# The pooling mixer of a fused two-layer trunk: its steps, and those of the first half up blocks, listed in another order on four engines, with fewer products on zeros

## The chip, the cores and the metric

The kernel runs on one core of one Trainium2 chip, with one launch. The metric is the device time of an execution in microseconds (us), the median of several runs. Engines are called as the profile calls them: PE is TensorE (PEld its weight loads), DVE VectorE, ACT ScalarE, POOL GpSimd, SP the engine that issues the transfers.

## What is computed

A decoder trunk of two layers on x of 512 x 1024, in float32. Layer 0 mixes by causal average pooling over four windows, layer 1 by stick-breaking attention; each is followed by an MLP with squared ReLU. Only the mixer of layer 0 and the entry of its MLP matter here:

```python
POOL_WINDOWS = (2, 4, 8, 16)
def pool_mixer(h, w_grp, scale):
    ...                                   # per group of 256 channels: mean over the last w rows, minus h itself
    y = jnp.einsum('bsgc,gcd->bsgd', y, w_grp.astype(jnp.float32)).reshape(B, S, D)
    return (y * scale.astype(jnp.float32)).astype(h.dtype)
def sq_relu_mlp(h, w_up, w_down):
    u = jnp.matmul(h, w_up)
    return jnp.matmul(jnp.square(jax.nn.relu(u)), w_down)
    ...
        h = rms_norm(x, mix_pre_g[layer])
        ...
        x = x + rms_norm(m, mix_post_g[layer])
        h = rms_norm(x, mlp_pre_g[layer])
        x = x + rms_norm(sq_relu_mlp(h, w_up[layer], w_down[layer]), mlp_post_g[layer])
```

## The kernel before

The 512 rows are four tiles t = 0 to 3 of 128 rows; the 1024 channels are two halves h of 512, or eight blocks of 128. Every product with a weight is made of three products of split operands (a high and a low part of each), so that each weight and each activation passes through a copy on ACT (high) and a subtraction on DVE (low).

The mixer is written as single steps, and one list, MIX_ORDER, says in which order they are issued. Inside that list the tile scheduler is off for PE, ACT, DVE and POOL (`tc.manual_schedule`): each of the four executes its own instructions in the order of the list, and waits for the others by semaphores. SP, and everything behind the mixer, is ordered by the scheduler. A step is a letter and its arguments; `p02` is pooled(0, 2), `z3` is busy(3). The steps, with the line (of the kernel before) that the profile shows:

- `z` busy(n), L773, PE: n products of a tile of zeros (bf16, 128x512) into a bank that nobody reads.
- `r`/`e` scale_row, scale_copy, L778 PE and L781 ACT: the row of per-channel scales, spread over 128 partitions by a product with ones.
- `q`/`v` first squares of x[t] (L302, ACT) and the norm from them: two small POOL instructions, the total (L306) and the power of -1/2 (L313).
- `b` band, L810 DVE: the pooling matrices times that norm, into own[t].
- `p` pooled, L818 PE: x[t] times own[t], in three groups of blocks (3, 3 and 2); `c` its copy to y[t] on ACT (L828); `f` adds what reaches over from the tile before (L835 DVE).
- `w` linear, L789 DVE: scales into the group maps; `m` mixed, L846 PE: y[t] times the map.
- `s`/`g` squares of the mixer's output (L302 ACT) and its product with the gain (L350 DVE); `V` the norm (L306, L313 POOL); `a` the update of x[t] (L368 DVE); `S` squares of the new x[t] (L302 ACT); `W` its norm (L306, L313 POOL); `n` the normed x (L404 DVE); `t` four transposes (L412 PE); `h`/`l` the high and low part of the transposed tile, xnh (L422 ACT) and xnl (L431 DVE).
- `i`/`k` the high and low part of one of the first four up weights (L863 ACT, L867 DVE); `u` half_up: the first half of an up block, for tiles 0 and 1 alone, which needs their xnh and xnl and both parts of the weight.

```python
        def busy(n):
            for _ in range(n):
                nc.tensor.matmul(pwarm, warm[:, :P], warm, start=True, stop=True)
        def half_up(j):
            early.append((ps(), left.pop(("L", j))[1]))
            up_block(*early[j], slice(0, S // 2))
    ...
        for k in ks:                                     # up_block: 8 x 3 products of 128x256
            nc.tensor.matmul(pu[:, cols], wh[:, k, :], xnh[:, k, cols], start=k == 0, stop=False)   # L728
            nc.tensor.matmul(pu[:, cols], wh[:, k, :], xnl[:, k, cols], start=False, stop=False)    # L729
            if not last:
                low(k)                                                                              # L725
    ...
            for step, which in MIX_ORDER:
                steps[step](*which)
```

Behind the list the MLP of layer 0 begins: the second halves of the four up blocks (for tiles 2 and 3), then the down projection (L606) with the further up blocks between its products.

Of the kernel before, what the change touches and what calls it, by code (L numbers as in the profile page):

```python
# [43 lines left out]

MIX_ORDER = [
    (w[0], [int(w[1:])] if w[0] == "z" else [int(c) for c in w[1:]])
    for w in """z13 q00 q01 v0 r1 b0 q1 z3 p02 p00 v1 c02 e1 r0 c00 p01 b1 e0 p12 w0 c01 p10 c12 p11 c10 w1 m00 q2
    m01 c11 v2 s00 f10 f11 b2 q3 p21 g00 p22 s01 v3 g01 m11 c22 V0 b3 c21 f21 m10 a00 i0 g11 s11 k0 p32
    s10 p31 g10 m21 c32 c31 V1 a01 S00 f31 a11 p20 S01 a10 p30 S11 W0 m31 g21 S10 n00 c20 W1 c30 t00 f20
    n01 m20 s31 n10 h00 n11 i1 t01 l00 t11 s20 t10 f30 g31 m30 h10 k1 h01 h11 l01 s30 l10 s21 l11 i2 V3  # L50
    z6 u0 V2 g30 i3 a31 a21 S31 a30 S21 u1 g20 S30 a20 W3 S20 k2 n30 u2 W2 n31 n21 n20 t21 k3 t31 h21
    t30 h31 t20 l21 u3 h30 l31 h20 l30 l20""".split()
]


# [56 lines left out]
def trunk(ctx, tc, x, consts, grow, pw, wup, wdn, wq, wk, wv, wo, out):  # L112
    nc = tc.nc
# [623 lines left out]
    with tc.tile_pool(name="mix0", bufs=1, reuse_waits="tile") as mp:  # L737
# [29 lines left out]
        left, stats, ups, ys, own = {}, {}, {}, {}, {}  # L767
# [101 lines left out]
        def half_up(j):  # L869
# [5 lines left out]
            "b": band, "p": pooled, "c": copied, "f": reached, "m": mixed,  # L875
            "s": lambda t, h: ups[t].squares_of(h, left["m", t, h]),
            "g": lambda t, h: ups[t].product(h, left["m", t, h]),
            "V": lambda t: ups[t].first_rstd(), "a": lambda t, h: ups[t].add_part(h),
            "S": lambda t, h: ups[t].squares_of_x(h), "W": lambda t: ups[t].rstd(),
            "n": lambda t, h: ups[t].norm_part(NS[h]), "t": transposes,  # L880
# [473 lines left out]
```

## Time and profile before

| | before |
|---|---|
| device time, three runs | 946.4, 946.53, 947.62 us; median 946.53 |
| the profiled execution | 947.41 us, of which the span of its instructions is 945.6 us |
| mean granted PE clock | 0.998 |
| PE busy | 936.8 us, 99% of the span, 4702 matmuls |
| DVE, ACT, POOL busy | 696.3 (74%), 560.0 (59%), 41.1 us (4%) |
| bytes moved | 156.15 MB, 46.0% of the 16 DMA engines' span |

The span counts from the first instruction to the last; 1.8 us of the profiled execution lie around it. The mixer and the half up blocks take the first 48 us of the span. Matmuls are pipelined, so that a row's duration is longer than its distance to the next row; on PE the distances between starts are what one product costs.

### The profile page before, as it was taken

To read this page: it belongs to the slowest core of one execution; us is meant where nothing else is said; L and a number is where in the kernel's file an instruction comes from. 1 tells how busy PE (TensorE), PEld (TensorE's weight loads), DVE (VectorE), ACT (ScalarE), POOL (GpSimd) and SP (SyncE) were. 2 spreads that over 40 slices of the span, in tenths; PEclk is the share of its full clock that TensorE was granted. 3 is DMA by queue.
4 is the path that set the end of the run, shared out by engine and by line. 5 is a ranking of instruction groups with operands and counts; after the bars stand their busy time and mean duration, and the time that the engine had idled before them with its cause. 6 is when DMAs were issued, how large, how long until landed. Compare 5 with 4: busy or idle time off the path is not lost.

```text
span 945.6 us, 12346 instructions
## 1 busy us (share of the span) xinstructions
PE 936.8 (99%) x4702; PEld 789.7 (84%) x4702; DVE 696.3 (74%) x797; ACT 560.0 (59%) x983; POOL 41.1 (4%) x83
## 2 busy tenths in 40 slices
PE   9999999999999999999999999999999999999996
PEld 7998888888888888888889888898888888888885
DVE  5865799988978976268766388884696966858756
ACT  6667979788784647155545464875545444444532
POOL 2300000000000004000000001200000000000002
PEclk9999999999999999999999999999999999999999
DMA  8254969789597860633151271342514233133102
GB/s 301 96 189 132 353 212 350 292 277 364 215 322 267 292 217 2 222 134 134 63 178 73 103 276 45 138 153 91 175 45 148 75 133 112 47 132 112 42 3 90
DMA packets 43262, 156.15 MB, mean 165 GB/s; under 512 B 4289, under 2 KB 4673, under 8 KB 43202
## 3 DMA queue, kind: packets, MB, share of 16 engines
q1 hardware_dynamic: 43202, 155.36, 46.0%
q8 instruction: 37, 0.61, 0.3%
q14 instruction: 23, 0.19, 0.1%
HBM read 121.79 MB, written 33.55 MB: 164 GB/s over the span
## 4 chain that ended last, share of the span: by engine, by line
PE 97%; POOL 1%; ACT 1%; DVE 1%; issue 0%; POOLq 0%; DVEq 0%; ACTq 0%
PE ps L606 28%; PE ps L728 15%; PE ps L725 15%; PE ps L729 15%; PE ps L317 4%; PE ps L318 4%; PE ps L319 4%; PE ps L1063 2%; PE ps L1046 2%; PE ps L1088 2%; PE ps L846 1%; PE ps L412 1%; PE ps L818 1%; PE ps L773 1%; ACT xn L302 1%; DVE x L368 0%
## 5 line engine op out<-in xcount | busy, mean ns | idle before, releaser
L606 PE MATMUL ps<-w,a 128*128 128x512 f32 x1176 | 278.6, 389 | 0.0
L728 PE MATMUL ps<-xnh,w 128*128 128x512 f32 (+1 forms) x704 | 260.5, 372 | 0.0
L729 PE MATMUL ps<-xnl,w 128*128 128x512 f32 (+1 forms) x704 | 259.9, 370 | 0.0
L725 PE MATMUL ps<-xnh,w 128*128 128x512 f32 (+1 forms) x704 | 259.2, 370 | 0.1
L606 PEld LDWEIGHTS ps<-w,a 128*128 128x128 f32 x1176 | 220.7, 188 | 45.9 <-DVE w L299 0.2
L729 PEld LDWEIGHTS ps<-xnl,w 128*128 128x128 f32 x704 | 132.7, 189 | 22.2
L725 PEld LDWEIGHTS ps<-xnh,w 128*128 128x128 f32 x704 | 132.2, 188 | 22.9 <-DVE w L867 0.3
L728 PEld LDWEIGHTS ps<-xnh,w 128*128 128x128 f32 x704 | 132.3, 188 | 22.4
L615 DVE TENSOR_TENSOR y<-ps,y 128x512 f32<-128x512 f32 x124 | 84.5, 688 | 44.3 <-PE ps L606 44.2
L178 DVE TENSOR_TENSOR w<-raw,w 128x1024 fp32r<-128x1024 f32 x58 | 70.9, 1223 | 57.1 <-ACT w L176 56.9
L176 ACT CAST w<-raw 128x1024 fp32r<-128x1024 f32 x58 | 60.8, 1048 | 81.9 <-PE ps L725 80.9
L298 ACT CAST a<-r 128x768 fp32r<-128x768 f32 (+1 forms) x60 | 47.6, 794 | 71.8 <-PE ps L606 55.4
L299 DVE TENSOR_TENSOR a<-r,a 128x768 fp32r<-128x768 f32 (+1 forms) x60 | 54.1, 902 | 11.9 <-ACT a L298 11.6
L1027 DVE TENSOR_TENSOR_SCAN e<-u,begin 128x1280 f32<-128x1280 f32 x16 | 45.2, 2825 | 20.9 <-ACT u L1011 20.2
L298 ACT CAST w<-e 128x1536 fp32r<-128x1536 f32 (+1 forms) x30 | 41.8, 1395 | 23.1 <-DVE e L580 13.7
L299 DVE TENSOR_TENSOR w<-e,w 128x1536 fp32r<-128x1536 f32 (+1 forms) x30 | 49.5, 1649 | 1.8 <-ACT w L298 1.6
L188 ACT ACTIVATE apart<-apart,eye 128x128 f32<-128x128 f32 (+1 forms) x132 | 43.1, 407 | 0.0
L299 DVE TENSOR_TENSOR w<-w,w 128x1536 fp32r<-128x1536 f32 (+1 forms) x20 | 33.0, 1650 | 8.0 <-ACT w L298 7.2
L638 ACT ACTIVATE r<-ps 128x512 f32<-128x512 f32 x56 | 33.0, 589 | 9.0 <-PE ps L725 9.0
L299 DVE TENSOR_TENSOR w<-xn,w 128x1536 fp32r<-128x1536 f32 (+1 forms) x20 | 33.0, 1650 | 5.6 <-ACT w L298 5.5
L639 ACT ACTIVATE r<-r 128x512 f32<-128x512 f32 x56 | 35.5, 633 | 1.3
L302 ACT ACTIVATE xn<-y 128x512 f32<-128x512 f32 (+1 forms) x25 | 15.3, 613 | 32.2 <-DVE y L484 28.6
(134 smaller groups left out, 1327.5 us busy)
## 6 DMA issues: line engine op xcount, KB each, us to landing
raw<-in_wup SPq DMA_DIRECT2D x64, 512.0 KB, 4.1
w<-kept SPq DMA_DIRECT2D x60, 512.0 KB, 4.1
kept<-wx SPq DMA_DIRECT2D x30, 512.0 KB, 4.9
w<-in_wdn SPq DMA_DIRECT2D x8, 1536.0 KB, 6.7
kept<-apart SPq DMA_DIRECT2D x24, 512.0 KB, 5.7
xn<-in_wdn SPq DMA_DIRECT2D x8, 1536.0 KB, 7.5
apart<-in_wk SPq DMA_DIRECT2D x7, 512.0 KB, 7.2
apart<-in_wq SPq DMA_DIRECT2D x7, 512.0 KB, 9.3
```

Of the source, the lines that this page charges most:

```text
L176: nc.scalar.copy(hi, raw)
L178: nc.vector.tensor_tensor(out=lo, in0=raw, in1=hi.bitcast(F32), op=ALU.subtract)
L188: nc.scalar.mul(c, c, gc[:, at : at + 1])
L298: latest["act"] = nc.scalar.copy(hi, src)
L299: latest["dve"] = nc.vector.tensor_tensor(out=lo, in0=src, in1=hi.bitcast(F32), op=ALU.subtract)
L317: nc.tensor.matmul(dst, ah, bh, start=start, stop=False)
L606: nc.tensor.matmul(bank, a[:, x, q, TS[t]], w[:, z, q], start=start and q == 0 and k == 0, stop=q == self.n - 1 and k == 2, skip_group_che ...
L615: nc.vector.tensor_tensor(out=part, in0=bank, in1=part, op=ALU.add)
L725: nc.tensor.matmul(pu[:, cols], wl[:, k, :], xnh[:, k, cols], start=False, stop=k == KC - 1)
L728: nc.tensor.matmul(pu[:, cols], wh[:, k, :], xnh[:, k, cols], start=k == 0, stop=False)
L729: nc.tensor.matmul(pu[:, cols], wh[:, k, :], xnl[:, k, cols], start=False, stop=False)
L1027: nc.vector.tensor_tensor_scan(out=self.e[:, ::-1], data0=self.u[:, 1:][:, ::-1], data1=begin[:, ::-1], initial=0.0, op0=ALU.mult, op1=ALU ...
```

## The change

MIX_ORDER holds the same steps in another order, and of its three steps on zeros, `z13`, `z3` and `z6`, only one is left, `z11`. Two more steps, X and Y, are defined (totals on DVE in place of POOL), but the list doesn't use them. The list is one line shorter and the two definitions are two lines longer, so line numbers differ by one.

```diff
-    for w in """z13 q00 q01 v0 r1 b0 q1 z3 p02 p00 v1 c02 e1 r0 c00 p01 b1 e0 p12 w0 c01 p10 c12 p11 c10 w1 m00 q2
...
+    for w in """z11 q00 r1 q01 v0 r0 q1 b0 v1 p00 b1 p01 p02 e0 e1 c01 c00 w0 w1 c02 p10 c10 q2 p12 q3 p11 m00 v2 s00 b2 c11 f10
...
+            "X": lambda t: (ups[t].first_total(nc.vector), ups[t].first_rstd()),
+            "Y": lambda t: (ups[t].second_total(nc.vector), ups[t].rstd()),
```

The first place is PE from its first products with data to the first product of tile 1. In the names, ps is a bank of the accumulator, row and ones make the scale row, own_ and x_ with x_70 are tile 0, with x_71 tile 1. Before:

```order
L778 MATMUL ps_143<-row,ones 128x512
L773 LDWEIGHTS warm
L773 MATMUL ps_110<-warm 128x512
L773 LDWEIGHTS warm
L773 MATMUL ps_110<-warm 128x512
L773 LDWEIGHTS warm
L773 MATMUL ps_110<-warm 128x512
L818 MATMUL ps_153<-own_145,x_70 128x144 x2
L818 MATMUL ps_156<-own_145,x_70 128x144 x3
L778 MATMUL ps_165<-row,ones 128x512
L818 MATMUL ps_168<-own_145,x_70 128x144 x3
L818 MATMUL ps_175<-own_172,x_71 128x144 x2
```

The same place now:

```order
L777 MATMUL ps_138<-row,ones 128x512
L777 MATMUL ps_143<-row,ones 128x512
L817 MATMUL ps_152<-own_148,x_70 128x144 x3
L817 MATMUL ps_158<-own_148,x_70 128x144 x3
L817 MATMUL ps_162<-own_148,x_70 128x144 x2
L817 MATMUL ps_179<-own_156,x_71 128x144 x3
```

The three products on zeros are gone, and both halves of the scale row stand ahead of the pooling of tile 0; what stands ahead of the first product of tile 1 is otherwise the same.

The second place is PE at the end of the mixer, up to the first half up block. L846 (L845 now) is a mixed product, with y_243 or y_231 of tile 2 and y_277 of tile 3; L412 (L411) are the transposes of tiles 0 and 1. Before, of the six products on zeros the first alone is shown:

```order
L846 MATMUL ps39_302<-pw1_98,y3_277 128x256 x4
L412 MATMUL ps40_314<-eye_74,xn3_79 128x128 x4
L846 MATMUL ps41_321<-pw0_97,y2_243 128x256 x4
L412 MATMUL ps42_331<-eye_74,xn3_79 128x128 x4
L412 MATMUL ps43_337<-eye_74,xn3_79 128x128 x4
L412 MATMUL ps44_343<-eye_74,xn3_79 128x128 x4
L846 MATMUL ps45_350<-pw0_97,y3_277 128x256 x4
L773 LDWEIGHTS warm_85
L773 MATMUL ps3_110<-warm_85 128x512
```

And now:

```order
L845 MATMUL ps38_303<-pw1_98,y2_231 128x256 x4
L411 MATMUL ps39_316<-eye_74,xn3_79 128x128 x4
L411 MATMUL ps40_322<-eye_74,xn3_79 128x128 x4
L845 MATMUL ps42_333<-pw1_98,y3_277 128x256 x4
L411 MATMUL ps43_340<-eye_74,xn3_79 128x128 x4
L411 MATMUL ps44_348<-eye_74,xn3_79 128x128 x4
L845 MATMUL ps45_353<-pw0_97,y3_277 128x256 x4
L727 MATMUL ps46_374<-xnh_80,w5_113 128x256
```

Tile 2 is done with its mixed products before the first transposes, and the first half up block follows the last mixed product of tile 3 at once.

The third place is the update and norm of tiles 2 and 3 on DVE, whose normed x the last transposes wait for. x2_72 and stat34 or stat36 are tile 2, x3_73 and stat38 or stat41 tile 3, w7, w9 and w11 are low parts of the up weights of blocks 1, 2 and 3. Before:

```order
L350 TENSOR_TENSOR m3_300<-ps45_350,grow1_104 128x512
L368 SCALAR_TENSOR_TENSOR x3_73<-m3_300,stat38_301,x3_73 128x512
L368 SCALAR_TENSOR_TENSOR x2_72<-m2_270,stat34_271,x2_72 128x512
L368 SCALAR_TENSOR_TENSOR x3_73<-m3_300,stat38_301,x3_73 128x512
L350 TENSOR_TENSOR m2_270<-ps41_321,grow1_104 128x512
L368 SCALAR_TENSOR_TENSOR x2_72<-m2_270,stat34_271,x2_72 128x512
L867 TENSOR_TENSOR w9_119<-raw8_117,w9_119 128x1024
L404 SCALAR_TENSOR_TENSOR xn_299<-x3_73,stat38_301,spare2_106 128x512 x2
L404 SCALAR_TENSOR_TENSOR xn3_79<-x2_72,stat34_271,spare2_106 128x512 x2
```

And now:

```order
L349 TENSOR_TENSOR m3_331<-ps45_353,grow1_104 128x512
L367 SCALAR_TENSOR_TENSOR x2_72<-m2_291,stat36_292,x2_72 128x512
L866 TENSOR_TENSOR w7_116<-raw6_114,w7_116 128x1024
L349 TENSOR_TENSOR m3_331<-ps42_333,grow1_104 128x512
L367 SCALAR_TENSOR_TENSOR x3_73<-m3_331,stat41_332,x3_73 128x512 x2
L403 SCALAR_TENSOR_TENSOR xn3_79<-x2_72,stat36_292,spare2_106 128x512 x2
L403 SCALAR_TENSOR_TENSOR xn_330<-x3_73,stat41_332,spare2_106 128x512 x2
L866 TENSOR_TENSOR w11_122<-raw10_120,w11_122 128x1024
```

Tile 2 is normed before tile 3 (before, after it), and the low part of block 1's weight has moved in between, while that of block 2 now stands far ahead. On PE the transposes of tile 2 now stand behind two half up blocks and those of tile 3 behind the third, where before all four stood behind the third:

```order
L724 MATMUL ps47_401<-xnh_80,w7_116 128x256
L411 MATMUL ps48_432<-eye_74,xn3_79 128x128 x4
L411 MATMUL ps49_438<-eye_74,xn3_79 128x128 x4
L727 MATMUL ps50_443<-xnh_80,w9_119 128x256
L728 MATMUL ps50_443<-xnl_81,w9_119 128x256
```

These rows are PE's now, at the end of the second half up block; ps47 is the bank of block 1, ps50 that of block 2.

On POOL the rows of the two orders are the same ones, with the pair for tile 2 and the pair for tile 3 exchanged. On SP one transfer of down weights has moved two places forward. Behind the mixer nothing else has moved but one pair of neighbours on ACT and a few rows on DVE at the start of the down projection.

More of the change, by code (lines that the diff above doesn't have):

```diff
@@ L46 @@
     (w[0], [int(w[1:])] if w[0] == "z" else [int(c) for c in w[1:]])
-    for w in """z13 q00 q01 v0 r1 b0 q1 z3 p02 p00 v1 c02 e1 r0 c00 p01 b1 e0 p12 w0 c01 p10 c12 p11 c10 w1 m00 q2
[L48 to L52, printed above, removed]
+    for w in """z11 q00 r1 q01 v0 r0 q1 b0 v1 p00 b1 p01 p02 e0 e1 c01 c00 w0 w1 c02 p10 c10 q2 p12 q3 p11 m00 v2 s00 b2 c11 f10
+    m01 v3 p21 p20 c12 s01 b3 c21 V0 p22 f11 c20 m10 g01 g00 m11 p32 c22 a00 i0 i2 a01 s10 f20 s11 k0 p31 S00 k2
+    S01 p30 c30 g11 g10 V1 W0 a11 f21 a10 c32 n01 S11 m20 c31 n00 S10 f31 s20 m21 s21 W1 g20 g21 f30 V2 t01 n10
+    t00 n11 h00 h01 m31 l01 a20 t10 s31 l00 h10 t11 m30 l10 h11 S20 i1 l11 g30 s30 a21 S21 V3 k1 W2 g31 a30 u0
+    a31 i3 u1 n21 n20 S30 S31 W3 t21 n31 t20 u2 n30 t30 h20 k3 h21 t31 l21 h30 l20 l30 h31 l31 u3""".split()
 ]
```

## The prediction

> **What bounds the kernel now.** I read the page first, for the engine that is full and for the chain that ended last.
>
> ```profile
> PE 936.8 (99%) x4702; PEld 789.7 (84%) x4702; DVE 696.3 (74%) x797; ACT 560.0 (59%) x983; POOL 41.1 (4%) x83
> PE 97%; POOL 1%; ACT 1%; DVE 1%; issue 0%; POOLq 0%; DVEq 0%; ACTq 0%
> ```
>
> PE is busy for 99% of the span and is 97% of the chain. Busy PE is not PE at work on data, so the next view is the table by stretches, for PE alone, cut at the places where the list changes (length of the stretch, then PE busy).
>
> ```profile
> core 0: us, PE busy (x), PEclk, DMA share, GB/s
> 1.30:6.82 5.52, 5.52 (x13) 1.00 0.83 269
> 6.82:7.84 1.02, 1.02 (x3) 1.00 1.00 384
> 7.84:8.49 0.65, 0.65 (x5) 1.00 1.06 401
> 9.71:10.57 0.86, 0.86 (x4) 1.00 1.02 419
> 32.75:33.86 1.11, 1.11 (x8) 1.00 0.72 151
> 8.00:65.00 57.00, 56.95 (x390) 1.00 0.53 199
> 65.00:938.00 873.00, 872.84 (x4299) 1.00 0.46 162
> ```
>
> From 8 us to 938 us PE is idle for 0.05 + 0.16 = 0.21 us. So whatever PE time leaves the first 48 us moves all that follows forward by as much, unless PE then waits for something that the products on zeros now hide. Nothing behind the mixer waits for a fixed moment; transfers there start when buffers come free, and move along. The question is therefore a sum over PE in the first 48 us: zeros out, new waits in.
>
> **The zeros.** The timeline of PE at the start gives their price (start, length, what).
>
> ```profile
> 1.30 5.73 PE L773 MATMUL ps<-warm 128*128 128x512 bf16 x13 [1.30 <-POOL warm L739]
> 6.82 1.18 PE L778 MATMUL ps<-row,ones 128*128 128x512 f32 x2
> 7.84 0.81 PE L773 MATMUL ps<-warm 128*128 128x512 bf16 x3
> 8.49 1.39 PE L818 MATMUL ps<-own,x 128*128 128x144 f32 x10
> 9.71 1.02 PE L778 MATMUL ps<-row,ones 128*128 128x512 f32 x2
> 10.57 1.63 PE L818 MATMUL ps<-own,x 128*128 128x144 f32 x12
> ```
>
> The first thirteen take 5.52 us, 0.425 each; the next three take 0.65, 0.217 each. PE thus runs at half speed at first. The first product of the scale row takes 1.02 us and the second 0.86: the excess of 0.16 is half of 0.32 us at half speed, so the speed doubled near 6.82 + 0.32 = 7.14, 5.84 us after the first product. (The column of the granted clock reads 1.00 throughout and does not show it.)
>
> `z13` to `z11` takes out 2 x 0.425 = 0.85 us. If the speed still doubles at 7.14, that much of the scale row runs at half speed instead, so half remains: 0.43. `z3` gives 0.65. `z6` gives the 1.11 us of its stretch. Together 2.19 us, the most that the zeros can bring.
>
> **What the zeros hid at the start.** The next PE work is the pooling of tile 1, which needs own1. Its chain, from the timeline of the other engines:
>
> ```profile
> 7.62 1.06 ACT L302 ACTIVATE junk<-x 128x1024 f32<-128x1024 f32 x1 [2.72 <-DMA x<-in_x]
> 9.25 0.56 POOL L313 TENSOR_TENSOR stat<-stat,mhalf 128x1 f32<-128x1 f32 x1
> 9.85 0.52 DVE L810 TENSOR_SCALAR own<-band,stat 128x576 f32<-128x576 f32 x1 [3.35 <-POOL stat L313]
> ```
>
> It begins with the landing of x for tile 1 and ends at 9.85 + 0.52 = 10.37; the new order moves nothing ahead of it. Before, PE came to tile 1 at 10.57 plus six of the twelve rows (6 x 0.1225 = 0.74), at 11.31. Now the same work stands ahead of it, less 0.43 and 0.65: 10.23. So PE waits about 0.17 us for own1, and 0.91 of the 1.08 remain.
>
> **What z6 hid, and the waits that go.** PE's rows around the half up blocks; two starts that lie further apart than 0.12 us are a wait.
>
> ```profile
> 33.86 0.47 PE L728 MATMUL ps<-xnh,w 128*128 128x256 f32 x1
> 34.16 0.28 PE L729 MATMUL ps<-xnl,w 128*128 128x256 f32 x1
> 39.91 0.28 PE L729 MATMUL ps<-xnl,w 128*128 128x256 f32 x1
> 40.25 0.39 PE L725 MATMUL ps<-xnh,w 128*128 128x256 f32 x1
> 40.47 0.28 PE L728 MATMUL ps<-xnh,w 128*128 128x256 f32 x1
> 42.87 0.28 PE L725 MATMUL ps<-xnh,w 128*128 128x256 f32 x1
> 43.09 1.97 PE L412 MATMUL ps<-eye,xn 128*128 128x128 f32 x16
> ```
>
> From 40.47 to 42.87 twenty products take 2.40 us, 0.12 each, so a half block of 24 takes 2.88. At 34.16 PE waited 0.18 for the low part of the transposed tile 1, even behind six zeros. Without them that wait could grow by all of 1.11. But before, tile 0's second transpose also stood behind the mixed product in the middle, and ACT and DVE had three high and low parts left after the last transposes; now one group of transposes comes a mixed product earlier, and two parts remain. I take the same 0.18 as before, so no change, with bounds of 0 and +1.1. At 40.25 PE waited 0.22 for the low part of block 2's weight, which now stands far ahead, and at 43.09 0.10 for the normed x: 0.32 go. Block 1's weight has become the late one: it comes by the walk below at the moment when the second half block's third product wants it, for which I put 0.1.
>
> **The new wait: tile 2's norm.** Before, all transposes of tiles 2 and 3 stood behind three half blocks (8.6 us of cover); now those of tile 2 stand behind two. Prices for the walk, from the timelines of DVE, ACT and POOL:
>
> ```profile
> 34.13 0.68 DVE L350 TENSOR_TENSOR m<-ps,grow 128x512 f32<-128x512 f32 x1
> 38.31 0.75 DVE L368 SCALAR_TENSOR_TENSOR x<-m,stat,x 128x512 f32<-128x512 f32 x1
> 38.98 1.22 DVE L867 TENSOR_TENSOR w<-raw,w 128x1024 fp32r<-128x1024 f32 x1
> 40.95 2.74 DVE L404 SCALAR_TENSOR_TENSOR xn<-x,stat,spare 128x512 f32<-128x512 f32 x4 [0.76 <-POOL stat L313]
> 37.10 0.63 ACT L302 ACTIVATE xn<-x 128x512 f32<-128x512 f32 x1 [0.38 <-DVE x L368]
> 37.64 0.19 ACT L302 ACTIVATION_READ_ACCUMULATOR xn<-x 128x1 f32 x1
> 38.54 1.74 POOL L306 TENSOR_SCALAR stat<-stat 128x1 f32<-128x1 f32 x1 [2.31 <-ACT xn L302]
> 40.36 0.56 POOL L313 TENSOR_TENSOR stat<-stat,mhalf 128x1 f32<-128x1 f32 x1
> 40.91 0.30 POOL L306 TENSOR_SCALAR stat<-stat 128x1 f32<-128x1 f32 x1
> ```
>
> Let s be the start of the first half block. DVE has the last low part until s + 0.8, then L350 of tile 3 (0.68) to s + 1.5. ACT squares it (0.73 to the end of its second row), s + 2.2, and POOL's total of tile 3 can begin at s + 2.3. DVE then runs L368 of tile 2 and L867 of block 1, until about s + 3.25. The POOL rows show what that does: the same total takes 0.30 us at 40.91 and 1.74 at 38.54, where L368 and L867 ran beside it, and it ended at 40.28, just behind L867 (40.20). So the total ends at s + 3.35, the power (0.56) at s + 4.0. Now DVE runs the two L368 of tile 3 until s + 5.4, and POOL the total and power of tile 2. If these run undisturbed they are done by s + 5.0, and the first L404 runs from s + 5.4 to s + 6.15. If the total waits for one L368, it is done at 5.5 and L404 at 6.3; if for both, 6.2 and 7.0. PE reaches the transposes at s + 2 x 2.88 + 0.18 = s + 5.94. The wait is 0.2, 0.4 or 1.1, and the second group of four transposes waits some 0.2 more, because an L404 takes 0.68 and four transposes less. I take 0.6 + 0.2 = 0.8, between the ends 0.4 and 1.3.
>
> [...]
>
> The transposes of tile 3 have a further half block of cover, and I count nothing for them.
>
> **Edits at no cost.** X and Y are never called. The first two up weights of the MLP (L166) wait for the buffers that the split of blocks 0 and 1 frees:
>
> ```profile
> 31.88 0.33 SPq L166 DMA_DIRECT2D raw<-in_wup  x1
> 51.70 1.04 ACT L176 CAST w<-raw 128x1024 fp32r<-128x1024 f32 x1
> ```
>
> The second one goes out at 31.88, and queued behind it on SP are the loads of the down weights. With block 1's split later, it goes out some 3 us later; its user, ACT at 51.70 for the first of them, leaves more than 10 us. If that cover were gone, PE would wait for the rest of it.
>
> **The sum.** -2.19 + 0.17 - 0.32 + 0.1 + 0.8 = -1.44 us against the profiled execution of 947.41 (945.6 and 1.8 around it): 945.97. The median of the runs shown is 946.53, 0.88 below that execution, and the runs span 1.22 us. If profiling is what costs the 0.88, the forecast for a median is 946.53 - 1.44 = 945.09. If it is the moment at which PE's speed doubles, the median run had it earlier; then both orders come to tile 1 when own1 is ready, the 0.91 are lost, and -0.53 remains: 946.0. Between the two I forecast **945.7 us**.
>
> **The rivals.** About 0.2% (1.89 us) is what a measurement of this kernel can tell from no change, so faster is below 944.64 and slower above 948.42.
>
> *The speed doubles early in most runs.* Each microsecond earlier moves PE by half of it, so from 7.14 - 2 x 0.91 = 5.3 us on down PE reaches tile 1 before 10.4 in both orders, and the start brings nothing. With the wait for tile 2 at its upper end, 1.3, the sum is -0.53 + 0.5: 946.5. For it speaks the spread of the runs; against it the profiled 7.14. Chance 0.14, inside the 0.2%. [...]
>
> *The new waits do not come.* Own1 hidden because the speed rises late, the total of tile 2 undisturbed: -2.19 - 0.32 + 0.4 = -2.1, 944.4, faster. For it: most of POOL's totals run beside nothing that disturbs them, and the rows' waits at 40.25 and 43.09 were small although the same chains are long. Against: the walk puts L368 beside the total by construction. Chance 0.32.
>
> *PE loses its speed.* The zeros kept PE at work where it would wait. If the waits at the first half block and at tile 2's transposes make it fall to half speed once, for as long as it took to rise (5.84 us), that costs 2.9: 945.7 + 2.9 = 948.6, slower. [...] Chance 0.14. [...]
>
> That the zeros are not removed is excluded by the rows of the order.
>
> **How the numbers follow.** The forecast has 0.40, the early rise 0.14, the faster case 0.32, the slower one 0.14: faster 0.32, same 0.54, slower 0.14. The lower end is the median less everything, 946.53 - 2.19 - 0.32 = 944.0, with no new wait; the upper end is -0.53, with 0.5 more for tile 2 and 1.1 for the wait behind z6: 947.6. About 2 in 10 lie outside.
>
> **What would show it.** Right: PE's rows at the pooling of tile 1 start at 10.4 or later than its predecessors end; no wait at block 2's weight; a wait of 0.4 to 1.3 us ahead of the transposes behind the second half block, with a POOL total beside L367 that takes over 0.5; the first L606, which the chain shows at 64.91 before, 0.5 to 1.9 earlier, and the same distance at the end.
>
> ```profile
> 64.91 2.72 PE ps L606 x12
> ```
>
> Wrong: a distance between products of 0.24 us and not 0.12 after 10 us (the speed fell), a wait over 0.5 at the first half block, or a PE wait behind 65 us that was not there.

## The result, and the profile after

The changed kernel takes 945.92 us (median of 20 runs, 945.22 to 947.08). Before, measured beside it, takes 947.35 (20 runs, 946.4 to 947.8): the three runs shown at first, with their median of 946.53, had two of the shortest among them, and the profiled execution of 947.41 was the usual one. The ratio is 0.9986, with a 95% interval of 0.998 to 0.9992: a small gain, of 0.8 to 1.9 us. The profiled execution of after takes 945.7 us, its span 943.9.

The page of after, busy time and shares of the chain:

```profile
PE 934.5 (99%) x4691; PEld 788.0 (83%) x4691; DVE 696.4 (74%) x797; ACT 560.2 (59%) x983; POOL 40.5 (4%) x83
PE 97%; DMA 1%; DVE 0%; ACT 0%; POOL 0%; SPq 0%; issue 0%; POOLq 0%; DVEq 0%; ACTq 0%
```

PE by stretches, the first of the prediction's two (length, PE busy, clock, DMA share, GB/s):

```profile
8.00:65.00 57.00, 55.91 (x382) 1.00 0.53 200
```

And PE's waits in it (total, times, longest):

```profile
PE ps L817 <- DVE own L809: 0.9, 1, 0.9
```

A DMA has come into the chain, with 1%, and between 8 and 65 us PE now stands idle for 1.09 us where it was 0.05. The timelines of PE and DVE at the start of after show where:

```profile
1.30 4.71 PE L772 MATMUL ps<-warm 128*128 128x512 bf16 x11 [1.30 <-POOL warm L738]
5.84 1.88 PE L777 MATMUL ps<-row,ones 128*128 128x512 f32 x4
7.56 2.12 PE L817 MATMUL ps<-own,x 128*128 128x144 f32 x16
10.62 1.61 PE L817 MATMUL ps<-own,x 128*128 128x144 f32 x11 [0.93 <-DVE own L809]
10.04 0.52 DVE L809 TENSOR_SCALAR own<-band,stat 128x576 f32<-128x576 f32 x1 [3.14 <-DMA band<-in_consts]
```

The four scale products take 1.72 us to the next row, 0.43 each, so PE was at full speed before 5.84. The last of tile 0's sixteen poolings starts at 9.40, and tile 1's first could follow at 9.53; it starts at 10.62. PE waits 1.09 us for own1, and own1 waits for a transfer. The chain that ended last, in order of time, names it:

```profile
3.81 6.14 DMA band<-in_consts
10.04 0.53 DVE own L809
10.62 2.23 PE ps L817 x16
...
63.45 2.72 PE ps L605 x12
```

It is the load of the second set of pooling matrices (`bands[1]`, for tiles 1 to 3), issued at 3.81 behind the first group map and landed at 9.95. The first down product stands at 63.45, 1.46 earlier than before.

The second place, the transposes of tile 2 behind two half blocks, on PE, POOL and DVE of after:

```profile
38.14 0.28 PE L724 MATMUL ps<-xnh,w 128*128 128x256 f32 x1
38.55 1.29 PE L411 MATMUL ps<-eye,xn 128*128 128x128 f32 x8
34.50 1.14 POOL L305 TENSOR_SCALAR stat<-stat 128x1 f32<-128x1 f32 x1 [5.62 <-ACT xn L301]
36.27 0.30 POOL L305 TENSOR_SCALAR stat<-stat 128x1 f32<-128x1 f32 x1
36.66 0.84 POOL L312 TENSOR_TENSOR stat<-stat,mhalf 128x1 f32<-128x1 f32 x1
34.26 1.22 DVE L866 TENSOR_TENSOR w<-raw,w 128x1024 fp32r<-128x1024 f32 x1
36.32 1.42 DVE L367 SCALAR_TENSOR_TENSOR x<-m,stat,x 128x512 f32<-128x512 f32 x2 [0.24 <-POOL stat L312]
37.66 1.40 DVE L403 SCALAR_TENSOR_TENSOR xn<-x,stat,spare 128x512 f32<-128x512 f32 x2
```

From 38.14 to 38.55 lie 0.41 us where a product takes 0.12: a wait of 0.29. A second, of 0.20, lies inside the eight transposes, at 39.21: the first four take 0.66 instead of 0.46. DVE's L403, which makes the normed x, follows the two L367 at once, and these had waited 0.24 for the norm of tile 3 on POOL.

**All kernels by stretches.** In every trace the start of one row to the start of another cuts the span alike: the first pooling product of tile 1, the first down product, the last product, the end (the last column of lengths is from the last product to the end). In us:

| kernel | tile 1 starts | from there to the first down product | to the last product | to the end | time, median |
|---|---|---|---|---|---|
| before | 11.31 | 53.44 | 873.31 | 7.56 | 947.35 |
| after | 10.62 | 52.67 | 873.49 | 7.13 | 945.92 |
| after_again | 10.88 | 52.66 | 873.29 | 7.14 | 945.8 |
| zeros_alone | 10.78 | 53.61 | 873.29 | 7.55 | 947.04 |
| order_alone | 11.20 | 53.12 | 873.30 | 7.14 | 946.36 |
| z6_back | 10.68 | 53.21 | 873.76 | 7.14 | 946.3 |
| z3_back | 10.84 | 52.66 | 873.54 | 7.15 | 945.96 |
| band_first | 10.41 | 52.66 | 873.31 | 7.14 | 945.69 |
| tile2_early | 10.27 | 52.33 | 873.31 | 7.57 | 945.74 |
| both | 10.77 | 52.33 | 873.32 | 7.55 | 945.73 |
| x1_first | 9.95 | 52.35 | 873.27 | 7.56 | 945.38 |
| x1_halves | 9.88 | 53.07 | 873.28 | 7.51 | 945.71 |
| no_start_zeros | 12.15 | 52.58 | 873.31 | 7.15 | 946.32 |

The third column repeats to 0.01 us where the list from tile 1 on is the same and PE waits for own1 (52.66 to 52.67, and 52.33 in the two kernels with another list). Where PE doesn't wait for own1 it is 0.09 shorter (no_start_zeros 52.58 against 52.67, order_alone 53.12 against z6_back's 53.21): behind that wait the second product of tile 1 starts 0.22 us after the first, and not 0.12. The second column does not repeat, even for the same list. So one profile tells what happens between 11 and 64 us to a tenth, and the start only to some tenths. From before to after: -0.69 at the start, -0.77 in the middle, +0.18 behind it, -0.43 at the end.

The last two are not of one kind. The 0.18 goes with the execution, since after_again is the same kernel and has 873.29, as before has 873.31. The end goes with the list: it takes 7.13 to 7.15 in all seven kernels with the new order from tile 1 on, and 7.51 to 7.57 in the two with the old order and in the four with the edit of tile2_early. The medians of before and after part by 1.43. If the middle and the end, 0.77 + 0.43 = 1.20, are the same in all executions, 0.23 is left for the start: an estimate. For after_again, 1.2 below its own before, nothing is left. So the usual execution gained little at the start, less than the 0.69 of the two profiles.

### The profile page after: what moved, and what is told of

It reads as the page before. It is cut to its first block, busy times and chain, and to the rows that moved or that the text cites. A ratio compares the mean times of both kernels' runs of the same rounds, so it can differ in the third digit from the quotient of the medians.

```text
span 943.9 us, 12327 instructions
## 1 busy us (share of the span) xinstructions
PE 934.5 (99%) x4691; PEld 788.0 (83%) x4691; DVE 696.4 (74%) x797; ACT 560.2 (59%) x983; POOL 40.5 (4%) x83
## 4 chain that ended last, share of the span: by engine, by line
PE 97%; DMA 1%; DVE 0%; ACT 0%; POOL 0%; SPq 0%; issue 0%; POOLq 0%; DVEq 0%; ACTq 0%
PE ps L605 28%; PE ps L727 16%; PE ps L728 16%; PE ps L724 15%; PE ps L317 4%; PE ps L316 4%; PE ps L318 4%; PE ps L1064 2%; PE ps L1047 2%; PE ps L1089 2%; PE ps L845 1%; PE ps L411 1%; PE ps L817 1%; DMA band<-in_consts 1%; ACT xn L301 0%; DVE x L367 0%
```

## The experiments

All are timed in five rounds against before (947.0 for the first four, 947.17 for the next four, 947.28 for the last three). In their diffs only the steps around an edit are shown.

**after_again** is the changed kernel once more.

> The changed kernel once more, unaltered, as the measure for its neighbours. Its median over 20 runs was 945.92 us against 947.35 before. Expected again: 1.0 to 1.7 us below the kernel before, PE waiting 0 to 1.1 us for own1 at about 10.5 us, as the moment falls at which PE's speed doubles, and 0.3 to 0.7 us ahead of the transposes of tile 2.

945.8 us, ratio 0.9987 (0.9978 to 0.9996). Its start differs from that of the first profile:

```profile
1.30 4.16 PE L772 MATMUL ps<-warm 128*128 128x512 bf16 x11 [1.30 <-POOL warm L738]
10.88 1.37 PE L817 MATMUL ps<-own,x 128*128 128x144 f32 x9 [1.75 <-DVE own L809]
```

Eleven zeros took 4.16 us instead of 4.71, so the speed doubled near 4.6 and PE was ready for tile 1 at 8.97 instead of 9.53. Own1 began at 10.31, 0.27 later than in the first profile, so PE waited 1.92 us, and its being ready earlier brought nothing.

**zeros_alone**: the old order, with the zeros of the new one.

```diff
-    z13 q00 q01 v0 r1 b0 q1 z3 p02 ...  (old order; z6 ahead of u0)
+    z11 q00 q01 v0 r1 b0 q1 p02 ...     (old order; no z6)
```

> The old order with z11 and without z3 and z6: the zeros go, the order stays. If every product on zeros cost its PE time (0.43 + 0.65 + 1.11 us) whatever the order, this would be about 2.2 us faster than the kernel before, and faster than the changed one. If the zeros mostly stood where PE would have waited, PE now waits there itself: up to 1.1 us for own1 and some 0.8 more for the low part of tile 1 behind the last mixed product, 0.9 for the low part of block 2's weight, and 0.3 to 1.1 us of gain are left; it is then slower than the changed kernel by 0.3 to 1.0.

947.04 us, ratio 1.0 (0.9992 to 1.0009): nothing. What PE waits for in this run (total, times, longest):

```profile
PE ps L817 <- DVE own L809: 0.9, 1, 0.9
PE ps L728 <- DVE xnl L430: 0.6, 1, 0.6
PE ps L724 <- DVE w L866: 0.5, 1, 0.5
```

By distances of starts, counted as under z6_back below, PE waits 0.90 us for the low part of tile 1, where before had no wait, and 0.40 more at block 2's weight than before. That makes 1.30, just what the six products of `z6` take, and the middle is 0.17 longer without them: in the old order they only filled waits. This is less than either theory gave the zeros.

**order_alone**: the new order, with `z13`, and with `z3` and `z6` at places that answer to the old ones.

```diff
-    z11 q00 ...  v1 p00 b1 ...  a30 u0
+    z13 q00 ...  v1 z3 p00 b1 ...  a30 z6 u0
```

> The new order with the old zeros: z13, z3 ahead of the first pooling, z6 ahead of the first half block. If the order matters and the zeros only fill waits: 0.4 to 0.9 us faster than the kernel before, since all of PE's waits up to the half blocks are hidden and none is in the way. If the zeros are what the change gained: no faster than the kernel before (within 0.3 us).

946.36 us, ratio 0.9994 (0.9985 to 1.0002): about half of the gain, with an interval that takes in no change. The middle is 0.32 shorter than before's, which is what the old waits were put at, and the end 0.42 shorter. These two make 0.74, where the medians part by 0.64: the part of the gain that the order brings alone lies there, and none at the start.

**z6_back**: after, with `z6` alone put back.

```diff
-    g31 a30 u0
+    g31 a30 z6 u0
```

> The changed kernel with z6 put back ahead of the first half block. If these six products cost their 1.11 us: 1.1 us slower than the changed kernel. If they only fill waits that PE has anyway (0.3 to 0.4 for the low part of tile 1, 0.5 ahead of tile 2's transposes), 0 to 0.4 us slower, and both waits are gone from the profile.

946.3 us, ratio 0.9992 (0.9983 to 1.0001), 0.5 above after_again, and the middle 0.54 longer. Both waits behind it are gone (PE):

```profile
32.37 1.46 PE L772 MATMUL ps<-warm 128*128 128x512 bf16 x6
33.48 0.47 PE L727 MATMUL ps<-xnh,w 128*128 128x256 f32 x1
33.78 0.28 PE L728 MATMUL ps<-xnl,w 128*128 128x256 f32 x1
39.42 1.04 PE L411 MATMUL ps<-eye,xn 128*128 128x128 f32 x8
```

From 32.37 to 33.78 lie 1.41 us: six zeros of 0.216 and one product of 0.12, with no wait. The row at 33.48 is recorded 0.19 early. So `z6` costs 1.30, not the 1.11 of its stretch, and the 0.18 that I read as before's wait for the low part was none. In after, the same count (8 mixed products from 30.58 and one of 0.12 give 32.43, against 32.54, and 0.11 more behind it) gives a wait of 0.22. With the 0.49 at tile 2's transposes this takes 0.71 of the 1.30: 0.59 remain, and 0.54 were measured.

**z3_back**: after, with `z3` ahead of the pooling of tile 0.

```diff
-    v1 p00 b1 p01
+    v1 z3 p00 b1 p01
```

> The changed kernel with z3 put back ahead of the first pooling. If PE's first data work is bounded by own1, these 0.65 us cost nothing in a run in which PE waits for own1 by more than that, and all of it in a run in which the speed doubles late: 0 to 0.3 us slower in the median, PE's wait for own1 shorter by 0.65 in the profile. If zeros cost their time: 0.65 slower.

945.96 us, ratio 0.9985 (0.9977 to 0.9994), the same as after. Tile 1 starts at 10.84, inside the 10.27 to 10.88 of the seven profiles with `z11`, without `z3` and with x of tile 1 loaded in the old place. PE is ready at 10.26 here and still waits 0.57 for own1, so in this execution the 0.65 us of `z3` cost nothing; the median says the same.

**band_first**: after, with the load of the second bands ahead of the first group map.

```diff
-        nc.sync.dma_start(wpool[0], pw[0])
         nc.sync.dma_start(bands[1], consts[:, at + 4 * BW :])
+        nc.sync.dma_start(wpool[0], pw[0])
```

> The changed kernel with two loads exchanged: the pooling matrices of tiles 1 to 3 ahead of the first group map, whose load stands in front of them. In the profile of the changed kernel own1 began at 10.04 us, when these matrices landed, not when its norm was ready. If that landing is the bound, own1 comes 0.4 to 0.9 us earlier and the median falls by 0.3 to 0.7 us. If the norm of tile 1 is the bound, or the group map then comes too late, nothing is gained (within 0.2 us).

945.69 us, ratio 0.9985 (0.9976 to 0.9993). The releaser of own1 has changed as expected, and the moment by 0.2 alone (DVE, POOL and ACT; the last two rows are those of after):

```profile
9.84 0.52 DVE L809 TENSOR_SCALAR own<-band,stat 128x576 f32<-128x576 f32 x1 [3.38 <-POOL stat L312]
9.24 0.57 POOL L312 TENSOR_TENSOR stat<-stat,mhalf 128x1 f32<-128x1 f32 x1
7.61 1.06 ACT L301 ACTIVATE junk<-x 128x1024 f32<-128x1024 f32 x1 [2.76 <-DMA x<-in_x]
8.89 0.57 POOL L312 TENSOR_TENSOR stat<-stat,mhalf 128x1 f32<-128x1 f32 x1
7.26 1.06 ACT L301 ACTIVATE junk<-x 128x1024 f32<-128x1024 f32 x1 [1.96 <-DMA x<-in_x]
```

Now tile 1's norm comes last: it ends at 9.81, and own1 follows at 9.84. In after it ended at 9.46, and own1 stood 0.58 behind it for the matrices. So the edit took 0.55 out of the wait, and x of tile 1, which landed 0.35 later in this execution, took most of it back. Two chains end at own1, and which of them is last differs between executions: with the loads in the old order own1 stands 0.30 to 0.58 behind the norm in four profiles (after, after_again, order_alone, no_start_zeros) and 0.03 to 0.08, so that the norm binds, in five. Shortening one of them gains less than I had put on it.

**tile2_early**: after, with tile 2's second update and the squares of it ahead of tile 3's first product with the gain.

```diff
-    i1 l11 g30 s30 a21 S21 V3 k1 W2 g31 a30 u0
+    i1 l11 s30 a21 S21 g30 V3 k1 W2 g31 a30 u0
```

> The changed kernel with the update of tile 2 and its squares ahead of tile 3's product with the gain, and the low part of block 1's weight behind it; nothing else moves. If the wait ahead of tile 2's transposes is the chain of tile 3's total behind that low part on POOL, the wait of 0.3 + 0.2 us falls to 0.2 in all, and the median by 0.2 to 0.5 us. If what PE waits for there is DVE's own row of work, the wait stays.

945.74 us, ratio 0.9986 (0.9977 to 0.9995). The middle is 0.34 shorter: the wait ahead of the transposes is gone and 0.17 of the second is left (PE; the POOL row is the total of tile 3):

```profile
37.93 1.23 PE L410 MATMUL ps<-eye,xn 128*128 128x128 f32 x8
38.91 0.36 PE L726 MATMUL ps<-xnh,w 128*128 128x256 f32 x1
33.38 0.30 POOL L304 TENSOR_SCALAR stat<-stat 128x1 f32<-128x1 f32 x1 [4.83 <-ACT xn L300]
```

The total of tile 3 now runs ahead of the low part of block 1's weight and takes 0.30, not 1.14. Little of the gain reaches the median (945.74, against 945.96 of z3_back in the same rounds), since the end of this kernel is the long one: 0.34 is won in the middle and 0.44 lost behind the last product. What the median still gained would then lie at the start, which one profile can't show.

**both** of the last two.

> The two edits before this one together, as a version that may beat both kernels: 0.4 to 1.1 us below the changed kernel if both hold, about 945 us; no gain over the better of the two if they cover the same wait.

945.73 us, ratio 0.9984 (0.9975 to 0.9993). The middle is 52.33 and the end the long one, as in tile2_early. But tile 1 starts at 10.77, later than in either: x landed later in this execution, and own1 with it (DVE, PE).

```profile
10.19 0.52 DVE L808 TENSOR_SCALAR own<-band,stat 128x576 f32<-128x576 f32 x1 [2.98 <-POOL stat L311]
10.77 1.49 PE L816 MATMUL ps<-own,x 128*128 128x144 f32 x10 [1.27 <-DVE own L808]
```

**x1_first**: both, and the load of tile 1's x ahead of all bands, the bands ahead of the small constants.

```diff
+        nc.sync.dma_start(xt[1], x[TS[1], :])
         nc.sync.dma_start(bands[0], consts[:, at : at + 4 * BW])
-        nc.sync.dma_start(xt[1], x[TS[1], :])
+        nc.sync.dma_start(bands[1], consts[:, at + 4 * BW :])
         nc.sync.dma_start(eye, consts[:, :at])
-        nc.sync.dma_start(bands[1], consts[:, at + 4 * BW :])
```

> This is the version with both edits (band loaded first, tile 2's product ahead) and one more: the load of x for tile 1 goes out ahead of the bands of tile 0, and both bands ahead of the small constants. Theory (the start is set by the moment at which own1 is ready, and that by what lands): ACT's square of tile 1 begins about 0.8 us earlier (295 KB fewer ahead of it), own1 is ready near 9.7, and PE, which gets tile 0's bands later, comes to tile 1 at 9.7 to 9.9 instead of 10.3 to 10.9; the stretch from there to the first half up block stays 21.50 us and all gains 0.5 to 0.9: about 945.0. Rival (something later in the mixer is the bound): that stretch grows by as much, and the time stays at 945.7.

945.38 us, ratio 0.9984 (0.9975 to 0.9993): the lowest median of all. ACT's square of tile 1, the two own and PE's pooling in this run:

```profile
6.56 1.06 ACT L300 ACTIVATE junk<-x 128x1024 f32<-128x1024 f32 x1 [1.05 <-DMA x<-in_x]
7.31 0.52 DVE L808 TENSOR_SCALAR own<-band,stat 128x576 f32<-128x576 f32 x1 [5.35 <-DMA band<-in_consts]
8.79 0.52 DVE L808 TENSOR_SCALAR own<-band,stat 128x576 f32<-128x576 f32 x1 [0.96 <-POOL stat L311]
7.89 4.19 PE L816 MATMUL ps<-own,x 128*128 128x144 f32 x32
```

Own1 starts at 8.79 instead of 10.04, and PE runs through 32 pooling products without a wait: tile 1 starts at 9.95, by PE's own work. The middle, 52.35, is as long as in both (0.09 less behind no wait for own1, and 0.11 more for a new wait in the first transposes, at 26.71), so the gain at the start passes on. The last product comes 1.21 us earlier than in after, 0.67 of it from the start and 0.32 from the middle; the end, 0.43 longer than after's, takes a part back. Against after the times themselves do not part the two; against before both are faster.

**x1_halves**: both, with x of tile 1 loaded and squared in two halves, the bands behind it.

```diff
-    r0 q1 b0 v1
+    r0 q10 q11 b0 v1
```

> The version with both edits, with x of tile 1 loaded and squared in two halves, as tile 0 is, and its bands loaded right behind. Theory: the last square behind the landing is half as long, own1 is ready 0.4 us earlier, and the time falls by 0.4 us, to 945.3. Rival (x lands no earlier, since the halves take longer to issue, or the bands land last): no change from 945.7.

945.71 us, ratio 0.9983 (0.9975 to 0.9992). Tile 1 starts at 9.88, better than expected, but the middle is 0.74 longer than in both. Tile 2 has become late, by its own landing, as PE, DVE and ACT show:

```profile
15.61 2.20 PE L817 MATMUL ps<-own,x 128*128 128x144 f32 x16
14.99 0.52 DVE L809 TENSOR_SCALAR own<-band,stat 128x576 f32<-128x576 f32 x1 [1.54 <-POOL stat L311]
12.76 1.06 ACT L300 ACTIVATE junk<-x 128x1024 f32<-128x1024 f32 x1 [1.32 <-DMA x<-in_x]
```

By distances, PE waits 0.30 here and 0.24 in the first transposes (27.37); the rest of the 0.74 is spread over small distances up to there. In the kernel both, the square of tile 2's x began at 12.76 too, but tile 1 at 10.77, so that it was early enough; in x1_first it began at 12.10. A later transfer took the wait over, which neither theory had named.

**no_start_zeros**: after, without `z11`.

> The changed kernel without its last products on zeros. If the zeros' use is to bring PE to full speed before data comes: PE begins at half speed with the scale row when it lands (5.2 to 5.9), the speed doubles 4 to 6 us later, products of 0.86 and 0.245 us take the place of 0.43 and 0.1225, and PE comes to tile 1 at 10.9 to 12 instead of 10.3 to 10.9: 0.3 to 1.2 us more, 946.1 to 947.0. Rival (the speed comes at a moment of its own, whatever PE does): the rows of the scale product are 0.43 from the start, tile 1 begins at 10.3 to 10.9 as before, and the time stays at 945.8.

946.32 us (945.17 to 947.48), ratio 0.9991 (0.9982 to 1.0). What the zeros do for the speed shows on PE:

```profile
5.46 3.75 PE L777 MATMUL ps<-row,ones 128*128 128x512 f32 x4 [5.46 <-POOL stat L305]
9.01 3.18 PE L817 MATMUL ps<-own,x 128*128 128x144 f32 x15
```

The four scale products take 3.55 us to the next row, and the poolings stand 0.24 apart up to 11.41 and 0.12 from there. Tile 1 starts at 12.15, 1.3 to 1.5 behind the two profiles of after, and by PE's own work, since own1 is done at 10.91. In the twelve profiles with zeros at the start PE is at full speed by 7.14 at the latest; here it begins its work 4.16 us later and is at half speed until 11.4. The speed follows PE's own work, and the rival is out. That the median rises by 0.4 to 0.5 only, with a spread of 2.3 us, would fit a rise at other moments in other executions; one profile can't show it.

## Why the prediction was right, point by point

**The sum.** The forecast on record is 945.7, and after measures 945.92; the sum of -1.44 against the profiled execution gives 945.97. Both are closer than their terms deserve. The 945.7 takes only 0.83 from a median of 946.53 that was 0.82 too low, a matter of three runs; neither of the two reasons that I gave for the 0.88 between it and the profiled execution was needed, since that execution was the usual one. In the sum, up to the first down product, -1.46 came out, made of a start that brought 0.22 less than I put and a middle that brought 0.24 more. The two profiled executions part by 1.71 and the medians by 1.43, and 0.43 of the 1.71 lies at the end, for which I had put nothing. That these errors cancel is luck; that order and waits, and not the zeros alone, decide is what the sum had right.

**The start** (-0.43 - 0.65 + 0.17 = -0.91; measured -0.69). That own1 takes the place of the zeros was right; the wait was mis-sized, 0.17 for 1.09. PE was ready at 9.53 instead of 10.23, since the speed doubled near 5.7 and not at 7.14. And own1 was done 0.19 later: "the new order moves nothing ahead of it" is true of the instructions, but I followed own1 back to its norm alone. It has a second input, whose load landed at 9.95 in after. The chain I quoted showed the last releaser of one execution: in before the norm ended at 9.81 and own1 began at 9.85, with the matrices just landed, while in after own1 had to wait 0.58 behind its norm.

**The moment is not the kernel's.** With one order of loads own1 starts at 9.70 to 10.39 over nine profiles (before among them), and the speed doubles 3.0 to 5.8 us after the first zero over twelve. In half of those it comes at 4.25 to 4.82, before my 5.3, the condition of the first rival. That own1 then binds is shown: z3_back and after_again differ in the start by 0.04 for 0.65 of zeros. The rival's time of 946.5 did not come, as the medians of after show, since its wait of 1.3 for tile 2 was 0.49 and the end was shorter; but its claim that the start brings nothing in the usual execution fits the medians. No profile of before with an early rise was taken. An estimate comes from zeros_alone, which has the old order and an early rise: PE is ready at 9.69 there, 10.77 with two more zeros and `z3` at full speed, and tile 1 starts at 10.78 for own1. Before would then start near 10.8, within a tenth of after_again's 10.88, and the new start would gain nothing.

**z6** (-1.11 and no change in the wait behind it; measured -1.30 and 0.22, together -1.08). Both steps were off and cancelled: I took a stretch between two starts for a price, where six times the price of one, from the rows at 7.84, would have said 1.30, and the 0.18 too much came back as a wait that was none.

**The old waits** (-0.32) are gone, and the whole of order_alone's middle is shorter by 0.32. In part this is chance: by distances 0.47 went (two products at block 2's weight and two at the transposes started late), and 0.15 came, in the transposes of tiles 0 and 1 (30.09 and 30.25 in after), where I had counted nothing. **Block 1's weight** (+0.1) made no wait. **The transposes of tile 2** (+0.8, between 0.4 and 1.3; measured 0.29 + 0.20 = 0.49). The walk's places were right: tile 3's total ran beside L866 and took 1.14, the total of tile 2 stands beside L367. But it took only 0.30 us, and the power behind it, beside the L367 too, 0.84 for 0.56: of my three cases it was the first, 0.2, with 0.1 more. That a total ends with the DVE row beside it was my estimate, from the rows at 38.54 and 40.91 of before. In after the total of 1.14 ended at 35.64, 0.16 behind L866, but that of 0.30 began at 36.27, 0.05 ahead of the first L367, and ended at 36.57, while DVE was at the two L367 until 37.7; what decides between the two is not shown. The power's 0.28 more cost nothing, since it ended at 37.50, within the L367; what delayed the transposes was the 1.14 of tile 3, as tile2_early shows. So one sign that I had named for being right did not come, a total beside L367 that takes over 0.5, and the wait of 0.4 to 1.3 came as 0.29, or 0.49 with its second part.

**Behind 65 us** I counted nothing. The last product moved 0.18 less than the first down product, which after_again does not repeat; in all traces this stretch lies within 873.27 and 873.76, in no order that follows the edits. From the last product to the end it is 0.43 shorter, and this is a term that the sum lacked.

**The slower rival** did not come: PE stood still for 1.09 us in after and 1.92 in after_again, and from the second product behind the wait on they stand 0.12 apart, at full speed. Whether a longer stand would cost the speed, no run shows. **The faster rival** did not come either: own1 was not hidden, though the total of tile 2 did run undisturbed (0.30 us), its other condition.

## What to carry to other kernels

Work on zeros is dear only where nothing else is late: here 1.3 us of it in the old order were worth nothing, and in the new order, with better cover, 0.5; so remove fillers together with the waits that they fill, and price both. Follow every operand of the instruction that will bind next back to its transfer, not only the one that the profile names as the last releaser; where two chains end within some tenths of each other, shortening one shows the other. Compare small edits stretch by stretch: a median also holds stretches that the edit was not meant to touch, here 0.4 us at the end, as much as the edit of tile2_early won. At a start that loads bind, put the loads in the order of the chains that hang on them: that brought the bound work forward by 0.7 us in the trace, where zeros taken out had brought nothing.

## What was not expected of the hardware

The time from PE's first product to full speed was 2.95 us in the shortest case (z6_back, 1.30 to 4.25, on zeros) and 5.95 in the longest (no_start_zeros, 5.46 to 11.41, on data); with the same first eleven zeros it was 2.95 to 5.84, and in five profiles 3.0 to 3.3. What sets the moment is not shown. Standing still for 1.92 us cost no speed: from the second product behind it on, PE's products in after_again stand 0.12 us apart.

A load lands at a moment that differs by over half a microsecond between executions: with the same loads ahead of it, ACT's square of tile 1's x starts at 7.26 in after and at 8.03 in z3_back. The DMA engines are 0.90 busy from 5 to 8 us of after; PE's stretch behind that shows a DMA share of 1.02 and 404 GB/s:

```profile
8.00:11.20 3.20, 2.27 (x18) 1.00 1.02 404
```

From the end of DVE's last update to the end of the span it takes 3.0 to 3.1 us in some kernels and 3.4 to 3.5 in others (after: 940.85 to 943.9; before: 942.13 to 945.6). The output's five transfers are the same in all, and the last lands 2.0 us behind DVE's end in before and in after alike; 0.4 of the profiled difference of 1.7 us lies behind it. There SP runs its last instructions, two of them DRAINs in a row. Before and after, SP's closing rows (count, shortest, median and longest in ns, first and last start):

```profile
L1350 SPq DRAIN x3: 7/7/130, 944.4 to 945.2; - x3
L1351 SPq DRAIN x3: 7/7/22, 943.2 to 943.7; - x3
```

In the seven short kernels the second DRAIN starts 2.37 us behind DVE's end, in five of the long ones 2.67, and in x1_halves the first does at 2.56 instead of 2.32. The traces count 466 instructions of SP in each of the short kernels, 467 in the five and 468 in x1_halves, and the late one is in all six the 464th. So the end goes with SP's count of instructions, and the new list, which leaves SP one fewer than the old, shortened it as a by-product. Why SP is late at that place is not shown.
